# The branch behind the first attention, w_out beside the second: a hybrid transformer block on one core

## The chip, the cores and the metric

The kernel runs on one core of a Trainium2 chip. The metric is the time of one execution on the device in microseconds (us); the reported time is the median of several runs. The core has TensorE (PE, matmuls and transposes; PEld is its weight load), VectorE (DVE), ScalarE (ACT), GpSimd (POOL) and SyncE (SP, which only issues DMAs here; GpSimd issues some too). The engines run their own instruction streams and wait for each other by semaphores.

## The reference

One decoder block, 2048 tokens of width 1024, in fp32. Two head groups share one input projection, and their outputs go through one output projection:

```python
go = gla_chunked(gq, gk, gv, g_log)            # gated linear attention, 4 heads
go = from_heads(rms_norm(go, gla_norm)) * silu(g_og)
...
s1, s2 = (q_m @ k_m.T) * scale, causal         # two maps of each of 4 heads
p_diff = softmax(s1) - lam * softmax(s2)
do = from_heads(rms_norm(p_diff @ v, diff_norm) * (1 - lambda_init))
...
y = concat([go, do]) @ w_out
x = x + gate * rms_norm(y)
h = relu(modulate(rms_norm(x)) @ w_up) ** 2    # 4096 wide
x = x + gate2 * rms_norm(h @ w_down)
```

(Shortened; q, k have 64 columns for each map, v has 128.) The gated attention may use a short form where no gate decays too far; the kernel computes a flag from the data, and where it is set it runs a general form. In these inputs the flag is 0.

## The kernel before, in words

Every fp32 product is made of three matmuls on split operands (high x high, low x high, high x low). A weight is therefore split once: ScalarE casts its high part, VectorE subtracts it from the weight for the low part.

The first 800 us hold the normalisation, the input projections and the gated attention. Then come the two calls of the differential attention, written as a generator, `attention` (L175): the first (pool pA0, query blocks t = 0, 1 of 512 tokens), the second (pool pA1, t = 2, 3). A step is a head and 128 queries: score matmuls S (L218, two maps), their evacuation with the running minimum on VectorE (L223, and L226 for the masked block on the diagonal), exp on ScalarE (L236), the combination of the two maps on VectorE (L242), and two steps later the transposes PT (L267), their copy on ScalarE (L269) and the products O with V (L278). When a head's four steps are done, its norm runs (L293) and its transposes dps (L301) give the two-part result dmo, which goes to the DRAM tile mixS. The generator yields after each block of 512 keys: a step of t = 1 has two yields, of t = 2 three, of t = 3 four. S, PT and dps share four PSUM banks in turn, tag "C".

The order around the change is set by the program's order, by how many yields are run between other work (`run(at, n)`), and by a scheduler that moves instructions within the limits of their dependences; at a branch all instructions ahead of it stay ahead, and all behind it stay behind. The first attention's steps are run two yields at a time beside the last input projections (`AT0`); what is left of it stands behind the branch. The branch (L885) is the general gated attention. Not taken, each engine jumps to a join and first waits there for its own earlier instructions. Behind it w_out is loaded (eight tiles of 128x1024 by GpSimd's queue, L911, three buffers), and split (L920 on ScalarE, L921 on VectorE), with `WL` = 2 yields of the first attention ahead of each.

`out_proj` (L927) makes the output projection of a token tile (128 tokens): it loads mx from mixS (1 MB, L933, SP) and x (L935), then makes two halves of 8 x 3 matmuls Y (L943 to L945), with a yield after each three, and then the norm and the residual add (L948 to L963). `interleave` runs it beside attention by a rate (`RA` = 2 for the rest of the first attention, `RB` = 2 for 48 yields of the second, then `RC` = 1.5). Tiles go in the order `TOKS`; the first `TB` = 11 run beside attention, the other five behind it beside the loads and splits for the up projection. `prep_first` prepares the up projection's operand and is paced by the same count of steps.

Behind all this, from about 1310 us on, the up and the down projection of the MLP run; the change does not touch them.

Of the kernel before, what the change touches and what calls it, by code (L numbers as in the profile page):

```python
# [9 lines left out]
F32 = mybir.dt.float32  # L10
F32R = mybir.dt.float32r
# [3 lines left out]
ALU = mybir.AluOpType  # L15
# [4 lines left out]
P = 128  # L20
S = 2048
D = 1024
NK = D // P
NH = 4
# [10 lines left out]
AT0 = 2  # L35
GA1 = 4
WL = 2
RA = 2.0
RB = 2.0
RC = 1.5  # L40
GA0 = 22
# [8 lines left out]
def tile_hybrid_block(  # L50
# [3 lines left out]
    nc = tc.nc  # L54
# [12 lines left out]
    mixS = [dram.tile([P, 4, 2 * NH, 2, P], F32, name=f"mixS{t}") for t in range(NT)]  # L67
# [104 lines left out]
    finished = set()  # L172


    def attention(tlist, sb, pw, pb, pp, tags, kb_, vb_, lag):  # L175
        steps = [(t, h, j) for t in tlist for h in range(NH) for j in range(4)]
        heads, qts, tiles, outs, rsd = {}, {}, {}, {}, {}
        dmask = sb.tile([P, 512], F32, tag="dmask", name="dmask", bufs=1)
# [75 lines left out]
        def due():  # L254
            for e in [e for e in queue if e[0] <= tick[0]]:
                queue.remove(e)
                e[1](*e[2])
# [50 lines left out]
        n = len(steps)  # L308
        for s in range(n + lag):
            cur = steps[s] if s < n else None  # L310
            old = steps[s - lag] if s >= lag else None
            if cur is not None:
                for a in range(3):
                    load(steps[min(s + a, n - 1)])
                tiles[cur] = ([sb.tile([P, pw], F32, tag="P", name="P", bufs=pb) for _ in range(2)],
                              [sb.tile([P, 4], F32, tag="nm", name="nm", bufs=8) for _ in range(2)],
                              sb.tile([P, 2, 2], F32, tag="sums", name="sums", bufs=4))
            nq = cur[0] + 1 if cur is not None else 0
            np_ = old[0] + 1 if old is not None else 0
            for ci in range(max(nq, np_)):  # L320
                tick[0] += 1
                if ci < nq:
                    qk(cur, ci)
                due()
                if ci < np_:
                    turn(old, ci)
                yield
            if cur is not None:
                softmax(cur)
            if old is not None:  # L330
                del tiles[old]
        while queue:
            tick[0] += 1
            due()
            yield
# [6 lines left out]
    sb = c0.enter_context(tc.tile_pool(name="p0", bufs=2, side="left"))  # L342
    sg = cG.enter_context(tc.tile_pool(name="p0g", bufs=2, side="right"))
    cps = ExitStack()
    pp = cps.enter_context(tc.tile_pool(name="p0ps", bufs=1, space=PSUM))
# [100 lines left out]
    def run(g, n=None):  # L446

        while n is None or n > 0:
            if next(g, run) is run:
                return False  # L450
            n = None if n is None else n - 1
        return True
# [421 lines left out]
    cA = ExitStack()  # L874
    sa = cA.enter_context(tc.tile_pool(name="pA0", bufs=2, side="right", reuse_waits="tile"))
    atags = {"S": ("C", 4), "O": ("D", 2), "T": ("C", 4)}
    at = attention((0, 1), sa, 1024, 6, pp, atags, 3, 3, 2)
    while run(dp, 1):
        run(at, AT0)
    run(rest)  # L880
    c0.close()

    with tc.tile_pool(name="gc", bufs=1, side="left", reuse_waits="tile") as gc:
        flag = nc.values_load(fi[0:1, 0:1], min_val=0, max_val=P)
# [15 lines left out]

    c1 = ExitStack()
    sw = c1.enter_context(tc.tile_pool(name="p1w", bufs=2, side="left", reuse_waits="tile"))
    gtg = sw.tile([P, D], F32, tag="gtg", name="gtg", bufs=1)
    nc.gpsimd.dma_start(gtg, gtS[0].partition_broadcast(P))
    wohi, wolo, woraw = [], [], []

    def load_wo(k):
        raw = sw.tile([P, D], F32, tag="wx", name="woraw", bufs=3)  # L910
        nc.gpsimd.dma_start(raw, w_out[k * P:(k + 1) * P, :])  # L911
        woraw.append(raw)

    for k in range(3):
        load_wo(k)
    for k in range(NK):
        run(at, WL)
        wh = sw.tile([P, D], F32R, tag=f"wohi{k}", name="wohi", bufs=1)
        wl = sw.tile([P, D], F32R, tag=f"wolo{k}", name="wolo", bufs=1)
        nc.scalar.copy(wh, woraw[k])  # L920
        nc.vector.tensor_tensor(wl, woraw[k], wh.bitcast(F32), op=ALU.subtract)  # L921
        wohi.append(wh)
        wolo.append(wl)
        if k + 3 < NK:
            load_wo(k + 3)

    def out_proj(tiles):  # L927

        for tk in tiles:
            assert all((tk // 4, h) in finished for h in range(NH))  # L930
            mx = sw.tile([P, 2 * NH, 2, P], F32R, tag="mx", name="mx", bufs=2)
            for ks in (slice(0, 7), slice(7, 8)) if tk >= 12 else (slice(0, 8),):
                nc.sync.dma_start(mx[:, ks].bitcast(F32), mixS[tk // 4][:, tk % 4, ks])  # L933
            xt = sw.tile([P, D], F32, tag="wx", name="wxt", bufs=3)
            nc.sync.dma_start(xt, x[tk * P:(tk + 1) * P, :])  # L935
            yps = []
            ss = sw.tile([P, 2], F32, tag="wss", name="wss", bufs=2)
            for b in range(2):
                yp = pp.tile([P, 512], F32, tag=("C" if tk > 12 and tk % 2 else "A"), name="Y",
                             bufs=4 if tk > 12 and tk % 2 else 2)  # L940
                cs = slice(512 * b, 512 * b + 512)
                for k in range(NK):
                    nc.tensor.matmul(yp, mx[:, k, 0, :], wohi[k][:, cs], start=(k == 0), stop=False)  # L943
                    nc.tensor.matmul(yp, mx[:, k, 0, :], wolo[k][:, cs], start=False, stop=False)  # L944
                    nc.tensor.matmul(yp, mx[:, k, 1, :], wohi[k][:, cs], start=False, stop=(k == NK - 1))  # L945
                    yield
                junk = sw.tile([P, 512], BF16, tag="wjunk", name="wjunk", bufs=1)
                nc.scalar.activation(junk, yp, AF.Square, accum_out=ss[:, b:b + 1])  # L948
                yps.append(yp)
            s1 = sw.tile([P, 1], F32, tag="ws1", name="ws1", bufs=2)  # L950
            nc.vector.tensor_tensor(s1, ss[:, 0:1], ss[:, 1:2], op=ALU.add)
            r = rsqrt_col(sw, s1, 1, 1.0 / D, "wr")
            yt = sw.tile([P, D], F32, tag="wx", name="wyt", bufs=3)
            for b in range(2):
                cs = slice(512 * b, 512 * b + 512)
                nc.vector.scalar_tensor_tensor(yt[:, cs], yps[b], r, gtg[:, cs], op0=ALU.mult, op1=ALU.mult)
            eng = nc.vector if tk >= 11 else nc.gpsimd
            eng.tensor_tensor(xt, xt, yt, op=ALU.add)
            nc.gpsimd.dma_start(x1S[tk], xt)

            s2 = sw.tile([P, 1], F32, tag="ws2", name="ws2", bufs=2)
            nc.scalar.activation(yt, xt, AF.Square, accum_out=s2)
            r2 = rsqrt_col(sw, s2, 1, 1.0 / D, "wq")  # L963
            nc.vector.tensor_scalar(yt, xt, r2, None, op0=ALU.mult)
            nc.gpsimd.dma_start(xnS[tk // 8][:, tk % 8], yt.rearrange("p (k c) -> p k c", c=P))
# [6 lines left out]
    wdS = [dram.tile([P, 3, 512], F32, name=f"wdS{p}") for p in range(NP_)]  # L972

    TOKS = (0, 4, 1, 5, 2, 6, 3, 7) + tuple(range(8, 16))

    def prep_first(pool, tag):

# [28 lines left out]
            for _ in range(2):  # L1008
                yield


    TB = 11
    op = out_proj(TOKS[:TB])

    def interleave(at, first, rate, later, pre=None):


        due, i = 0.0, 0
        while run(at, 1):
            due += rate if i < first else later  # L1020
            while due >= 1.0:
                if len(wsteps) == 16 * TB or not ready(TOKS[len(wsteps) // 16]):
                    due = 0.0
                    break
                run(op, 1)
                wsteps.append(1)
                due -= 1.0
            if pre is not None:
                run(pre, 1)
            i += 1  # L1030

    wsteps = []

    def ready(tk):
        return all((tk // 4, h) in finished for h in range(NH))

    interleave(at, 0, RA, RA)
    cA.close()
    cA = ExitStack()
    sa = cA.enter_context(tc.tile_pool(name="pA1", bufs=2, side="right", reuse_waits="tile"))  # L1040
    at = attention((2, 3), sa, S, 6, pp, atags, 5, 5, 2)
    pre = prep_first(sa, "C")
    interleave(at, 48, RB, RC, pre)
    run(op)
# [53 lines left out]
    def fetch_op(m):  # L1098

        g, i = opseq[m]  # L1100
        hsrc[m] = [prep_tile("hsrc", [P, 2, 512]) for _ in range(2)]
        for kp in range(2):
            nc.sync.dma_start(hsrc[m][kp], hS[g][:, OP[i], 2 * kp:2 * kp + 2, :])
# [52 lines left out]

    op = out_proj(TOKS[TB:])
    fetch_op(0)
# [21 lines left out]
    pp = c3.enter_context(tc.tile_pool(name="p2ps", bufs=1, space=PSUM, reuse_waits="tile"))  # L1180
# [53 lines left out]
    n = len(usteps)  # L1234
    ready_ops = {}
    prep_todo = [(k, hf) for k in range(4) for hf in range(2)]
    for s, (g, c, wi, p) in enumerate(usteps):
        i = WORD[wi]
# [17 lines left out]
        nm, first = BANK[i]  # L1256
# [34 lines left out]
    pp = c4.enter_context(tc.tile_pool(name="p3ps", bufs=1, space=PSUM, reuse_waits="tile"))  # L1291
# [157 lines left out]
    banks = {}  # L1449
# [25 lines left out]
    for s in range(nd - TAIL):  # L1475
        if s + AHEAD < nd:
            ready_ops[s + AHEAD] = down_ops(s + AHEAD)
        i, p, gs = dsteps[s]
# [98 lines left out]
```

## Time and profile before

| what | us |
|---|---|
| median of 3 runs | 2572.22 |
| lowest, highest | 2565.59, 2573.88 |
| the profiled execution | 2572.86 |
| its span | 2570.7 |

The profiled execution's mean granted TensorE clock is 0.982. From about 801 to 1280 us the span holds what the change edits. In a row of a timeline stand the start, the duration, the engine, the line and the operation; in brackets the engine's idle time ahead of it and what ended it. A row of the windows has start and end, length, then the busy time of PE, PEld, DVE, ACT and POOL with the count of instructions, the granted clock of PE, the mean busy share of the 16 DMA engines, and GB/s. In rows of groups the busy time and the mean duration in ns stand first, then the idle time ahead of the group and what ended it.

### The profile page before, as it was taken

What the parts mean: (1) busy time and instruction counts of PE and PEld (TensorE: products, weight loads), DVE (VectorE), ACT (ScalarE), POOL (GpSimd) and SP (SyncE); (2) the same over time, 40 slices, a digit from 0 to 9 for tenths busy, and PEclk for the clock granted to TensorE, in tenths of its full rate; (3) what the DMA queues carried; (4) which work ended last, traced back from release to release, by engine and by line L of the source; (5) the groups of instructions that cost most, each with busy time, mean ns of one, the idle gap of its engine ahead of it and who ended that gap; (6) DMA issues with size and microseconds to landing.
All of it is one profiled execution on the core that took longest, in us unless ns stands there. A gap on an engine that the chain in (4) does not pass through costs nothing.

```text
span 2570.7 us, 35387 instructions
## 1 busy us (share of the span) xinstructions
PE 2457.0 (96%) x12532; PEld 2055.5 (80%) x12532; DVE 1589.8 (62%) x3111; ACT 1159.2 (45%) x2201; POOL 417.6 (16%) x638
## 2 busy tenths in 40 slices
PE   5999999999998899999999999999999999999998
PEld 4877788887787788888778888788888788788886
DVE  7536754347865677767576667766664445544756
ACT  4352224412545566556555555544553333222444
POOL 1011230003311123232012322212211000100000
PEclk8999999999999999999999999999999999999999
DMA  7354553244845667655565655734438767855856
GB/s 270 110 191 141 179 191 111 98 141 157 242 131 181 207 206 229 204 181 158 211 224 198 232 189 175 239 134 160 157 126 301 254 198 242 279 176 161 289 167 209
DMA packets 218791, 491.60 MB, mean 191 GB/s; under 512 B 24848, under 2 KB 78800, under 8 KB 217072
## 3 DMA queue, kind: packets, MB, share of 16 engines
q1 hardware_dynamic: 170000, 329.12, 40.5%
q0 software_dynamic: 48608, 160.16, 16.8%
q8 instruction: 100, 1.64, 0.3%
q14 instruction: 83, 0.68, 0.1%
HBM read 329.79 MB, written 159.39 MB: 190 GB/s over the span
## 4 chain that ended last, share of the span: by engine, by line
issue 34%; PE 23%; POOL 7%; DVE 2%; DMA 1%; ACT 1%; POOLq 0%; SPq 0%; DVEq 0%; ACTq 0%
PE dn L1440 5%; PE dn L1441 5%; PE dn L1442 4%; PE S L218 2%; PE O L278 2%; POOL uS L1222 2%; POOL uS L1191 2%; PE Y L945 1%; PE Y L944 1%; PE Y L943 1%; PE PT L267 1%; POOL wdS L1320 1%; POOL uS L1230 1%; ACT P L236 1%; DMA q<-qS 0%
## 5 line engine op out<-in xcount | busy, mean ns | idle before, releaser
L1440 PE MATMUL dn<-dnhi,uhi 128*128 128x512 f32 x880 | 344.5, 391 | 3.0 <-DVE du L1420 3.0
L1442 PE MATMUL dn<-dnhi,ulo 128*128 128x512 f32 x880 | 344.2, 391 | 2.0 <-DVE ulo L1369 2.0
L1441 PE MATMUL dn<-dnlo,uhi 128*128 128x512 f32 x880 | 344.1, 391 | 0.0
L1367 ACT CAST uhi<-us 128x1024 fp32r<-128x1024 f32 (+1 forms) x126 | 118.7, 944 | 357.9 <-PE dn L1441 341.4
L1369 DVE TENSOR_TENSOR ulo<-us,uhi 128x1024 fp32r<-128x1024 f32 (+1 forms) x126 | 137.0, 1087 | 158.6 <-ACT uhi L1367 158.3
L535 PE MATMUL projt<-hThi,whi 128*128 128x512 f32 x512 | 203.9, 398 | 1.1 <-DVE cols L420 0.6
L537 PE MATMUL projt<-hThi,wlo 128*128 128x512 f32 x512 | 201.5, 393 | 2.2 <-DVE wlo L476 2.2
L536 PE MATMUL projt<-hTlo,whi 128*128 128x512 f32 x512 | 201.4, 393 | 0.0
L1440 PEld LDWEIGHTS dn<-dnhi,uhi 128*128 128x128 f32 x880 | 165.9, 189 | 38.9 <-ACT dnhi L1366 2.8
L1442 PEld LDWEIGHTS dn<-dnhi,ulo 128*128 128x128 f32 x880 | 165.9, 189 | 37.6 <-DVE ulo L1369 2.4
L1441 PEld LDWEIGHTS dn<-dnlo,uhi 128*128 128x128 f32 x880 | 166.0, 189 | 35.3
L236 ACT ACTIVATE P<-P,nm 128x128 f32<-128x128 f32 (+15 forms) x128 | 153.7, 1202 | 48.8 <-DVE nm L226 46.1
L1145 ACT CAST wuhi<-wA 128x512 fp32r<-128x512 f32 x160 | 99.1, 619 | 165.3 <-PE upV L1264 67.0
L218 PE MATMUL S<-K,q 128*128 128x512 f32 (+3 forms) x640 | 169.5, 383 | 2.8 <-issue 1.5
L278 PEld LDWEIGHTS O<-V,PTs 128*128 128x128 f32 x1088 | 142.3, 193 | 25.4 <-ACT PTs L269 14.3
L278 PE MATMUL O<-V,PTs 128*128 128x128 f32 x1088 | 152.6, 281 | 7.9 <-ACT PTs L269 4.2
L550 PE MATMUL projn<-whi,hThi 128*128 128x256 f32 x512 | 150.5, 294 | 4.5 <-DVE cols L420 2.7
L1265 PE MATMUL upY<-hhi,wulo 128*128 128x512 f32 x384 | 151.9, 396 | 2.0 <-DVE wulo L1146 2.0
L1263 PE MATMUL upY<-hhi,wuhi 128*128 128x512 f32 x384 | 151.7, 395 | 0.0
L1264 PE MATMUL upY<-hlo,wuhi 128*128 128x512 f32 x384 | 151.4, 394 | 0.0
L552 PE MATMUL projn<-whi,hTlo 128*128 128x256 f32 x512 | 148.1, 291 | 0.3 <-DVE hTlo L168 0.3
L551 PE MATMUL projn<-wlo,hThi 128*128 128x256 f32 x512 | 148.2, 290 | 0.0
(334 smaller groups left out, 5713.9 us busy)
## 6 DMA issues: line engine op xcount, KB each, us to landing
us<-uS SPq DMA_DIRECT2D x94, 512.0 KB, 4.4
wA<-in_w_up_dram SPq DMA_DIRECT2D x128, 256.0 KB, 3.0
uS<-t POOLq DMA_DIRECT2D x128, 256.0 KB, 3.2
wraw<-in_w_in_dram SPq DMA_DIRECT2D x48, 512.0 KB, 4.6
uS<-c POOLq DMA_DIRECT2D x96, 256.0 KB, 3.1
K<-kS SPq DMA_DIRECT2D x40, 512.0 KB, 5.5
wds<-in_w_down_dram SPq DMA_DIRECT2D x78, 256.0 KB, 4.0
adaraw<-in_ada_w_dram SPq DMA_DIRECT2D x32, 512.0 KB, 4.1
```

What stands on the lines that cost most here:

```text
L218: nc.tensor.matmul(ps[:, :wd], qt[:, m, hl, qs], Kc[ci][:, m, :wd], start=(hl == 0), stop=(hl == 1))
L236: nc.scalar.activation(Ps[m][:, :width], Ps[m][:, :width], AF.Exp, scale=-1.0, bias=nms[m][:, t:t + 1], accum_out=sums[:, 0, m:m + 1])
L278: nc.tensor.matmul(outs[t, h][:, j, :], pt[:, kb % 4, :], Vc[g][:, kb % 4, :], start=(kb == 0), stop=(kb == nb - 1))
L535: nc.tensor.matmul(ps, whi[k][:, cs], hi[:, k, :], start=(k == 0), stop=False)
L536: nc.tensor.matmul(ps, whi[k][:, cs], lo[:, k, :], start=False, stop=False)
L537: nc.tensor.matmul(ps, wlo[k][:, cs], hi[:, k, :], start=False, stop=(k == NK - 1))
L1263: nc.tensor.matmul(ps, whi[:, k, :], hi[:, k, :], start=(first and k == 0), stop=False, skip_group_check=not first)
L1264: nc.tensor.matmul(ps, whi[:, k, :], lo[:, k, :], start=False, stop=False, skip_group_check=not first)
L1265: nc.tensor.matmul(ps, wlo[:, k, :], hi[:, k, :], start=False, stop=(k == 3), skip_group_check=not first)
L1440: nc.tensor.matmul(banks[t], uhi[:, tk], whi, start=first, stop=False, skip_group_check=on)
L1441: nc.tensor.matmul(banks[t], uhi[:, tk], wlo, start=False, stop=False, skip_group_check=on)
L1442: nc.tensor.matmul(banks[t], ulo[:, tk], whi, start=False, stop=last, skip_group_check=on)
```

## The change

All steps of the first attention are run ahead of the branch; only its queued end (the last products, the norm and the store) is left behind it. The pool of the second attention is opened right behind that, and the loads and splits of w_out are spread over the second attention's first 16 yields, where cast, subtraction and the first matmul of the output projection are kept in the order of the program. All 176 steps of the first eleven token tiles now run beside the second attention; before, the first tile's 16 ran beside the first. The load of mx goes through `load_mx`, one tile ahead of its use, x is loaded halfway through its tile, and for the last four tiles mx is loaded by GpSimd's queue. The PSUM banks of Y are "C" for tile 11, too (before: 13 and 15 only).

```diff
-RA = 2.0
...
-    def attention(tlist, sb, pw, pb, pp, tags, kb_, vb_, lag):
+    def attention(tlist, sb, pw, pb, pp, tags, kb_, vb_, lag, ends):
...
+        ends.append(tlist)
         while queue:
             tick[0] += 1
             due()
...
+    while not ends:
+        run(at, 1)
 
     with tc.tile_pool(name="gc", bufs=1, side="left", reuse_waits="tile") as gc:
         flag = nc.values_load(fi[0:1, 0:1], min_val=0, max_val=P)
...
+    run(at)
+    cA.close()
+    cA = ExitStack()
     c1 = ExitStack()
...
+    sa = cA.enter_context(tc.tile_pool(name="pA1", bufs=2, side="right", reuse_waits="tile"))
+    at = attention((2, 3), sa, S, 6, pp, atags, 5, 5, 2, ends)
+    run(at, 1)
     for k in range(3):
         load_wo(k)
     for k in range(NK):
         run(at, WL)
...
-        nc.scalar.copy(wh, woraw[k])
-        nc.vector.tensor_tensor(wl, woraw[k], wh.bitcast(F32), op=ALU.subtract)
+        tc.keep_in_program_order(nc.scalar.copy(wh, woraw[k]))
+        tc.keep_in_program_order(nc.vector.tensor_tensor(wl, woraw[k], wh.bitcast(F32), op=ALU.subtract))
...
+    def load_mx(tk):
+
+        if tk in mxs or not ready(tk):
+            return
+        mxs[tk] = sw.tile([P, 2 * NH, 2, P], F32R, tag="mx", name="mx", bufs=2)
+        eng = nc.gpsimd if tk >= 12 else nc.sync
+        for ks in (slice(0, 7), slice(7, 8)) if tk >= 12 else (slice(0, 8),):
+            eng.dma_start(mxs[tk][:, ks].bitcast(F32), mixS[tk // 4][:, tk % 4, ks])
+
     def out_proj(tiles):
 
         for tk in tiles:
-            assert all((tk // 4, h) in finished for h in range(NH))
-            mx = sw.tile([P, 2 * NH, 2, P], F32R, tag="mx", name="mx", bufs=2)
-            for ks in (slice(0, 7), slice(7, 8)) if tk >= 12 else (slice(0, 8),):
-                nc.sync.dma_start(mx[:, ks].bitcast(F32), mixS[tk // 4][:, tk % 4, ks])
-            xt = sw.tile([P, D], F32, tag="wx", name="wxt", bufs=3)
-            nc.sync.dma_start(xt, x[tk * P:(tk + 1) * P, :])
+            load_mx(tk)
+            mx = mxs.pop(tk)
+            banks = ("C", 4) if tk >= 11 and (tk - TB) % 2 == 0 else ("A", 2)
...
-                yp = pp.tile([P, 512], F32, tag=("C" if tk > 12 and tk % 2 else "A"), name="Y",
-                             bufs=4 if tk > 12 and tk % 2 else 2)
+                yp = pp.tile([P, 512], F32, tag=banks[0], name="Y", bufs=banks[1])
                 cs = slice(512 * b, 512 * b + 512)
                 for k in range(NK):
-                    nc.tensor.matmul(yp, mx[:, k, 0, :], wohi[k][:, cs], start=(k == 0), stop=False)
+                    mm = nc.tensor.matmul(yp, mx[:, k, 0, :], wohi[k][:, cs], start=(k == 0), stop=False)
+                    if (tk, b, k) == (0, 0, 0):
+                        tc.keep_in_program_order(mm)
...
+                    if (b, k) == (1, 0):
+
+                        xt = sw.tile([P, D], F32, tag="wx", name="wxt", bufs=3)
+                        nc.sync.dma_start(xt, x[tk * P:(tk + 1) * P, :])
+                        for nx in TOKS[TOKS.index(tk) + 1:TOKS.index(tk) + 2]:
+                            load_mx(nx)
                     yield
...
+    def op_step():
+
+        if len(wsteps) == 16 * TB or (len(wsteps) % 16 == 0 and TOKS[len(wsteps) // 16] not in mxs):
+            return False
+        run(op, 1)
+        wsteps.append(1)
+        return True
...
+            n = len(wsteps) // 16
+            if len(wsteps) % 16 == 0 and n < TB and TOKS[n] not in mxs:
+                load_mx(TOKS[n])
+                asked[n] = i
             while due >= 1.0:
-                if len(wsteps) == 16 * TB or not ready(TOKS[len(wsteps) // 16]):
+                n = len(wsteps) // 16
+                if (len(wsteps) % 16 == 0 and i < asked.get(n, -3) + 3) or not op_step():
                     due = 0.0
                     break
-                run(op, 1)
-                wsteps.append(1)
                 due -= 1.0
...
-    interleave(at, 0, RA, RA)
-    cA.close()
-    cA = ExitStack()
-    sa = cA.enter_context(tc.tile_pool(name="pA1", bufs=2, side="right", reuse_waits="tile"))
-    at = attention((2, 3), sa, S, 6, pp, atags, 5, 5, 2)
+    load_mx(0)
     pre = prep_first(sa, "C")
     interleave(at, 48, RB, RC, pre)
```

**SyncE's DMAs.** Before, SyncE (L206 is q, L933 mx, L196 V, L194 K, L935 x) has these rows behind the branch: the first mx and the last loads of the first attention, and then the second attention's K, V and q (kS_60, vS_64 and qS_62), which the scheduler moved into the first attention's time.

```order
L885 UNCONDITIONAL_BRANCH x2
L206 DMA q<-qS_63 64x2x256
L933 DMA mx<-mixS_78 128x2048
L196 DMA V<-vS_65 128x4x128
L194 DMA K<-kS_61 128x2x512
L206 DMA q<-qS_63 64x2x256 x4
L196 DMA V<-vS_65 128x4x128
L935 DMA wxt<-in_x_dram 128x1024 x2
L194 DMA K<-kS_60 128x2x512
L196 DMA V<-vS_64 128x4x128
```

In the change (L952 is mx, L193 K, L195 V, L205 q) the same place of SyncE reads:

```order
L889 UNCONDITIONAL_BRANCH x2
L952 DMA mx<-mixS_78 128x2048
L193 DMA K<-kS_60 128x2x512
L195 DMA V<-vS_64 128x4x128
L193 DMA K<-kS_60 128x2x512
L195 DMA V<-vS_64 128x4x128
L193 DMA K<-kS_60 128x2x512
L195 DMA V<-vS_64 128x4x128
L205 DMA q<-qS_62 64x2x256 x8
```

The loads of the first attention have moved ahead of the branch; the second attention's K, V and q now come right behind the join and the first mx.

**TensorE, the start of the second attention.** Before, TensorE has at the change from the first attention to the second: the last products of the first, its last dps, two steps of scores, and then the output projection's second token tile.

```order
L278 MATMUL O<-V,PTs 128x128 x8
L301 MATMUL dps<-ident,don 128x128 x4
L218 MATMUL S<-K,q 128x512 x8
L218 MATMUL S<-K,q 128x128 x4
L218 MATMUL S<-K,q 128x512 x8
L218 MATMUL S<-K,q 128x256 x4
L218 MATMUL S<-K,q 128x512
L943 MATMUL Y<-wohi,mx 128x512
L944 MATMUL Y<-wolo,mx 128x512
L945 MATMUL Y<-wohi,mx 128x512
```

In the change TensorE has at this place, right behind the join:

```order
L889 UNCONDITIONAL_BRANCH x2
L277 MATMUL O<-V,PTs 128x128 x5
L300 MATMUL dps<-ident,don 128x128 x4
L217 MATMUL S<-K,q 128x512 x8
L217 MATMUL S<-K,q 128x128 x4
L217 MATMUL S<-K,q 128x512 x8
L217 MATMUL S<-K,q 128x256 x4
L217 MATMUL S<-K,q 128x512 x4
L266 MATMUL PT<-ident,P 128x128 x4
L217 MATMUL S<-K,q 128x512 x4
```

The branch now stands ahead of the first attention's last five products, and no Y follows the first two steps of scores. The first Y of the change comes some fifty such rows later on TensorE, behind the scores of the sixth step:

```order
L217 MATMUL S<-K,q 128x512 x4
L277 MATMUL O<-V,PTs 128x128 x3
L266 MATMUL PT<-ident,P 128x128 x4
L217 MATMUL S<-K,q 128x512 x4
L277 MATMUL O<-V,PTs 128x128 x4
L266 MATMUL PT<-ident,P 128x128 x4
L217 MATMUL S<-K,q 128x256 x4
L277 MATMUL O<-V,PTs 128x128 x4
L266 MATMUL PT<-ident,P 128x128 x4
L966 MATMUL Y<-wohi,mx 128x512
L969 MATMUL Y<-wolo,mx 128x512
L970 MATMUL Y<-wohi,mx 128x512
```

Between the second attention's first scores and its first Y there are now only its own matmuls; VectorE has the eight subtractions of w_out (L931) among its work for the same steps.

More of the change, by code (lines that the diff above doesn't have):

```diff
@@ L876, in tile_hybrid_block @@
     atags = {"S": ("C", 4), "O": ("D", 2), "T": ("C", 4)}
-    at = attention((0, 1), sa, 1024, 6, pp, atags, 3, 3, 2)
+    ends = []
+    at = attention((0, 1), sa, 1024, 6, pp, atags, 3, 3, 2, ends)
     while run(dp, 1):
@@ L925, in tile_hybrid_block, with ready @@
             load_wo(k + 3)
+    TOKS = (0, 4, 1, 5, 2, 6, 3, 7) + tuple(range(8, 16))
+    TB = 11
+    mxs = {}
+    def ready(tk):
+        return all((tk // 4, h) in finished for h in range(NH))
+    def load_mx(tk):
[5 more added lines that the diff above has]
+            eng.dma_start(mxs[tk][:, ks].bitcast(F32), mixS[tk // 4][:, tk % 4, ks])
     def out_proj(tiles):
         for tk in tiles:
-            assert all((tk // 4, h) in finished for h in range(NH))
-            mx = sw.tile([P, 2 * NH, 2, P], F32R, tag="mx", name="mx", bufs=2)
-            for ks in (slice(0, 7), slice(7, 8)) if tk >= 12 else (slice(0, 8),):
-                nc.sync.dma_start(mx[:, ks].bitcast(F32), mixS[tk // 4][:, tk % 4, ks])
-            xt = sw.tile([P, D], F32, tag="wx", name="wxt", bufs=3)
-            nc.sync.dma_start(xt, x[tk * P:(tk + 1) * P, :])
+            load_mx(tk)
+            mx = mxs.pop(tk)
+            banks = ("C", 4) if tk >= 11 and (tk - TB) % 2 == 0 else ("A", 2)
             yps = []
@@ L972, in tile_hybrid_block @@
     wdS = [dram.tile([P, 3, 512], F32, name=f"wdS{p}") for p in range(NP_)]
-    TOKS = (0, 4, 1, 5, 2, 6, 3, 7) + tuple(range(8, 16))
     def prep_first(pool, tag):
@@ L1009, in prep_first, with interleave @@
                 yield
-    TB = 11
     op = out_proj(TOKS[:TB])
-    def interleave(at, first, rate, later, pre=None):
-        due, i = 0.0, 0
+    wsteps = []
+    def op_step():
[4 more added lines that the diff above has]
+        return True
+    def interleave(at, first, rate, later, pre):
+        due, i, asked = 0.0, 0, {}
         while run(at, 1):
             due += rate if i < first else later
+            n = len(wsteps) // 16
+            if len(wsteps) % 16 == 0 and n < TB and TOKS[n] not in mxs:
+                load_mx(TOKS[n])
+                asked[n] = i
             while due >= 1.0:
-                if len(wsteps) == 16 * TB or not ready(TOKS[len(wsteps) // 16]):
+                n = len(wsteps) // 16
+                if (len(wsteps) % 16 == 0 and i < asked.get(n, -3) + 3) or not op_step():
                     due = 0.0
                     break
-                run(op, 1)
-                wsteps.append(1)
                 due -= 1.0
-            if pre is not None:
-                run(pre, 1)
+            run(pre, 1)
             i += 1
-    wsteps = []
-    def ready(tk):
-        return all((tk // 4, h) in finished for h in range(NH))
-    interleave(at, 0, RA, RA)
-    cA.close()
-    cA = ExitStack()
-    sa = cA.enter_context(tc.tile_pool(name="pA1", bufs=2, side="right", reuse_waits="tile"))
-    at = attention((2, 3), sa, S, 6, pp, atags, 5, 5, 2)
+    load_mx(0)
     pre = prep_first(sa, "C")
```

## Prediction

> **What bounds the kernel now.** I read the totals first, then the busy time by stretch around the edited code, then TensorE's own timeline there. The profiled execution took 2572.86 us with a span of 2570.7 us; the median shown is 2572.22, so sums made against this execution stand 0.6 us above the median.
>
> ```profile
> span 2570.7 us, 35387 instructions
> PE 2457.0 (96%) x12532; PEld 2055.5 (80%) x12532; DVE 1589.8 (62%) x3111; ACT 1159.2 (45%) x2201; POOL 417.6 (16%) x638
> ```
>
> TensorE (PE) is busy 96% of the span. The change leaves the count of matmuls as it is, so it can only win or lose PE's idle or slow-clocked time. The stretches show where that lies around the branch (columns: window, length, busy time of PE, weight loads, VectorE, ScalarE, GpSimd, granted clock, DMA share, GB/s).
>
> ```profile
> 801.50:863.30 61.80, 46.48 (x269) 38.86 (x269) 41.49 (x116) 38.31 (x93) 9.72 (x14) 0.88 0.72 231
> 863.30:875.00 11.70, 9.14 (x32) 7.40 (x33) 8.99 (x29) 5.66 (x8) 2.23 (x4) 0.75 0.64 227
> 875.00:1235.00 360.00, 350.68 (x2145) 304.36 (x2144) 263.79 (x762) 217.28 (x436) 95.17 (x116) 0.99 0.60 192
> 1050.00:1060.00 10.00, 7.61 (x31) 5.62 (x29) 9.75 (x28) 6.30 (x21) 2.93 (x2) 0.83 0.60 179
> 1135.00:1145.00 10.00, 7.95 (x40) 6.59 (x38) 7.05 (x19) 4.88 (x10) 1.10 (x2) 0.83 0.38 139
> ```
>
> From 875 to 1235 PE is busy 350.68 of 360 us at clock 0.99: with output-projection matmuls (Y) as filler, the second attention is bound by PE. From 801.5 to 863.3, the rest of the first attention with the split of w_out, it is busy 46.48 of 61.80 at clock 0.88. PE's timeline shows the waits in there.
>
> ```profile
> 804.78 0.76 PE L278 MATMUL O<-V,PTs 128*128 128x128 f32 x2 [3.23 <-PEq L885]
> ...
> 854.80 2.05 PE L278 MATMUL O<-V,PTs 128*128 128x128 f32 x16 [0.24 <-ACT PTs L269]
> 863.32 1.09 PE L301 MATMUL dps<-ident,don 128*128 128x128 f32 x4 [6.47 <-DVE don L293]
> 864.05 1.20 PE L218 MATMUL S<-K,q 128*128 128x512 f32 x2
> ...
> 874.37 0.50 PE L943 MATMUL Y<-wohi,mx 128*128 128x512 f32 x1 [2.38 <-DMA mx<-mixS]
> ```
>
> The branch costs 3.23 us; the last head's norm chain, between its last O and dps, 6.47. The first score matmuls (S) of the second attention follow dps at once: their loads had long landed. At 874.37 the second attention's first Y runs, with two steps of S behind it. That is my fixed point: I work out when the changed kernel reaches its first Y, and put the work that is then ahead or behind into microseconds of PE.
>
> **Part 1, the first attention alone.** In the change the six remaining steps of the first attention run before the branch, without Y and without the split. VectorE (DVE) sets their pace.
>
> ```profile
> L921 DVE TENSOR_TENSOR wolo<-woraw,wohi 128x1024 fp32r<-128x1024 f32 x8 | 9.7, 1218 | 2.1 <-ACT wohi L920 2.1
> L956 DVE SCALAR_TENSOR_TENSOR wyt<-Y,wrr,gtg 128x512 f32<-128x512 f32 x2 | 1.4, 746 | 0.0
> ```
>
> DVE is busy 41.49 us between 801.5 and 863.3. Less the eight split subtractions (9.7) and Y's evacuation (1.4) that is 30.4 for the first attention; about 2 of it is the last head's norm, which stays behind the branch. So 28.4 us from 801.5, then transposes, copy and O of the last step (about 1.5): 831.5 if DVE never idles. I take 833 for its idling; at the share of the row 863.30:875.00 (8.99 of 11.70) it would be 838. The branch itself goes nowhere: every engine still waits at the join for its own earlier work, 3.23 as before. The join is at about J = 836.
>
> **Part 2, from the join to the first S.** Before, K, V and q of the second attention were issued while the first one still ran:
>
> ```profile
> 843.71 0.54 SPq L194 DMA_DIRECT2D K<-kS  x1
> 844.30 0.59 SPq L196 DMA_DIRECT2D V<-vS  x1
> ```
>
> That is 20 us ahead of the S that used them (864.05). In the change they stand behind the branch on SyncE (SP), behind the first mx load, and GpSimd's queue issues gtg and three pieces of w_out at the same moment. Sizes and one full stretch:
>
> ```profile
> K<-kS SPq DMA_DIRECT2D x40, 512.0 KB, 5.5
> q<-qS SPq DMA_DIRECT2D x128, 128.0 KB, 4.5
> mx<-mixS SPq DMA_DIRECT2D x12, 1024.0 KB, 5.6
> V<-vS SPq DMA_DIRECT2D x40, 256.0 KB, 4.1
> woraw<-in_w_out_dram POOLq DMA_DIRECT2D x8, 512.0 KB, 6.5
> ...
> 815.00:820.00 5.00, 3.03 (x8) 1.92 (x8) 3.57 (x10) 4.16 (x6) 0.53 (x1) 0.80 0.99 342
> ```
>
> Ahead of the fourth piece of q, which S needs, SP has mx, three K, three V and four q: 1024+1536+768+512 = 3840 KB. GpSimd has three pieces of w_out and gtg, a 128x1024 fp32 tile like them: 2048 KB. At 342 GB/s, where the DMA share is 0.99, the 5888 KB (6.03 MB) take 17.6 us. From below, S cannot start before the norm chain has let dps go: O about 1.1, then 6.47, then 0.73 to the first S, so J+8. I take J+16, near the burst, because not all of GpSimd's bytes need to be ahead of q: 852. The ends J+8 and J+18 are kept.
>
> The Trainium skill (Trainium Kernel Development and Optimization, "Key Constraints") says that transfers issued from different engines' queues run on the same 16 DMA engines and interleave. It speaks against this change, which puts both queues' bursts at one point. Were the queues independent, SP's 3840 KB alone would take 11.5 us and the sum would be 4 us lower; with the rule it stands. The trace has no such burst of this size; its row above has both queues near saturation.
>
> **Part 3, the second attention without filler.** The w_out split now lies in its first 16 yields, and the first Y is held behind the scores of the sixth step. Until then PE has 72 S matmuls, 42 transposes and 38 products O.
>
> ```profile
> 876.56 0.39 PE L943 MATMUL Y<-wohi,mx 128*128 128x512 f32 x1
> 876.79 0.40 PE L944 MATMUL Y<-wolo,mx 128*128 128x512 f32 x1
> ...
> 888.08 1.08 PE L218 MATMUL S<-K,q 128*128 128x512 f32 x4
> 889.00 1.05 PE L278 MATMUL O<-V,PTs 128*128 128x128 f32 x8
> 889.89 0.60 PE L267 MATMUL PT<-ident,P 128*128 128x128 f32 x4
> 890.24 0.47 PE L943 MATMUL Y<-wohi,mx 128*128 128x512 f32 x1
> ```
>
> By the distances of these starts a Y takes 0.23 us, four S of 512 columns 0.92, four O (which the trace lists as eight) 0.89, four transposes 0.35. So 12 full yields of S make 11.0, the six partial ones 128+256+384+512+128+256 = 1664 columns, 3.0; O 8.5; transposes 3.7: 26 us of PE. DVE has more to do:
>
> ```profile
> L223 DVE TENSOR_SCALAR_CACHE_REDUCE P<-S,nm 128x512 f32<-128x512 f32 x10 | 7.2, 747 | 1.0 <-PE S L218 1.0
> L223 DVE TENSOR_SCALAR_CACHE_REDUCE P<-S 128x512 f32<-128x512 f32 x10 | 6.5, 689 | 6.2 <-PE S L218 6.1
> L242 DVE SCALAR_TENSOR_TENSOR P<-P,cf 128x1152 f32<-128x1152 f32 (+3 forms) x4 | 6.5, 1616 | 0.0
> L226 DVE CUSTOM_DVE_ANT_0 P<-S,dmask,nm 128x128 f32<-128x128 f32 (+3 forms) x8 | 4.1, 545 | 2.5 <-PE S L218 2.5
> L223 DVE DVE_READ_ACCUMULATOR P<-S 128x1 f32 x10 | 0.8, 83 | 0.0
> ```
>
> The last transposes ahead of Y take the bank of a score tile whose evacuation is 24th in DVE's order. Up to there: 12x0.747 + 12x0.689 = 17.2; 10x0.545 = 5.5; 34 accumulator reads at 0.083 = 2.8; five L242 at 1.616 = 8.1; five times some 0.5 of one-column work = 2.6; seven subtractions at 1.218 = 8.5. That is 44.7 us. The reads lie partly beside other work, DVE idles a little, so I take 45, from 43 to 58 (44.7 at the share 8.99/11.70). The first Y is at 852 + 45 = 897.
>
> By then the changed kernel is ahead in attention: 26.2 us of PE against the two steps of S done by 874.37 (4.4), so 21.8. It is behind by one token tile of Y, since before that tile ran beside the first attention: 48 x 0.23 = 11.0. Net 10.8 us, 11 at the pace of the long stretch (360/350.68). So 897 stands for 886, against 874.4: **11.6 us late**.
>
> **Part 4, the rest of the second attention and the tail.** Before, the Y tiles ended early and the attention's end ran without them; now they reach to its end, so nothing more is due later. Two holes may close.
>
> ```profile
> 1128.15 0.47 SPq L935 DMA_DIRECT2D wxt<-in_x_dram  x1
> ```
>
> ```profile
> 1134.71 1.06 ACT L962 ACTIVATE wyt<-wxt 128x1024 f32<-128x1024 f32 x1 [2.66 <-POOL wxt L958]
> ```
>
> In 1135:1145 PE lost 3.4 us (10 - 7.95x0.83). Just ahead of it ScalarE waited 2.66 us for a tile's residual add, whose x was asked for at 1128.15 only, late on SP behind the loads of mx and K; mx is now asked for a tile earlier, and x half a tile ahead of its use. In 1050:1060 it lost 3.7, where Y waits for banks. I take 2 back (ends 0 and 7). The tail's bank wait goes, since tile 11 takes other banks:
>
> ```profile
> 1252.99 0.79 PE L943 MATMUL Y<-wohi,mx 128*128 128x512 f32 x1 [2.80 <-DVE wyt L956]
> ```
>
> But tile 12 now fills the drain of the last head and follows tile 10 in the same banks. I take 2 back (0 to 2.8).
>
> **Sum:** 11.6 - 2 - 2 = +7.6, so 2572.9 + 7.6 = 2580.5; less the 0.6 to the median I say **2580**. Prefetching mx takes PE's 2.38 us wait at 874.37 away, but in the change that time lies inside the DVE-bound stretch, so I count it at nothing; if Y began earlier it would be worth that much.
>
> **Rivals.**
> First, *the loads hide*: S follows dps at J+8, as before. First Y 836+8+45 = 889, stands for 878, 3.6 late; less 4 it is -0.4: 2572.5. For it: 20 us of lead were more than needed, and K alone lands in 5.5. Against: SP serves mx first, and 5.9 MB at once.
> Second, *it really gains*: the same, DVE at 43, both holes and the tail wait closed: 836+8+43-11 = 876, 1.6 late, less 7 and 2.8: -8.2, or 2564.5. For it: those holes are waits that prefetching meets. Against: 1050:1060 is a bank wait with DVE busy 9.75 of 10, which the change doesn't touch.
> Third, *slower by more*: DVE idles in the unfilled stretch as it does in 863.30:875.00, since each S waits for a bank and each transpose for ScalarE, which also casts w_out: 58 instead of 45, +13 more: 2593. It decides as soon as DVE's share there is below 0.85. Against: with Y as filler the long stretch shows no such waits.
>
> The Trainium skill (TensorE: Matmul & The Clock Gate, "A second HAM failure mode: psum-queue depth-cycling") tells of PE dropping to half clock when it idles often and briefly while cycling through banks; by that the 26 us of PE would be 52 in the unfilled stretch, which also gives about 7 us more than my sum. Here clock 0.75 in 863.30:875.00 follows a long idle, so the trace leaves it open, and I count it under the third rival.
>
> **Chances.** The forecast (burst, DVE-bound start) 0.45; loads hidden 0.28; a real gain 0.12; slower by more 0.15. About 0.3%, 7.7 us, can be told from no change. The forecast's own range, +2 to +12, lies on both sides of that: 0.19 of it within, 0.26 above. Hence faster 0.12, same 0.28+0.19 = 0.47, slower 0.26+0.15 = 0.41. The range goes from the second rival's 2564 to just short of the third's 2593.
>
> **What would show it.** PE's timeline: the branch wait near 833 and still about 3 us; the first S of the second attention at least 12 us behind the join, released by a DMA (if by dps, the first rival); DVE's share above 0.9 from there to the first Y, PE's near 0.6; the first Y some 45 us after the first S; no 2.8 us wait at the tail. I am wrong if the first Y comes before 885 or if the stretch behind it loses much less than the 9.3 us idle of now.

## The result and the profile after

The change makes the kernel slower: a median of 2594.26 us (4 runs, 2589.53 to 2606.09) against 2570.4 us of before, ratio 1.0095 with a 95% interval of 1.0071 to 1.0119. Later, on another chip, it was 2597.45 against 2570.38, ratio 1.0117 (1.0100 to 1.0134). The forecast was 2580, its range 2564 to 2592.

The page of the changed kernel: the same matmuls, the same busy time of TensorE, a longer span.

```profile
span 2588.3 us, 35407 instructions
PE 2456.2 (95%) x12532; PEld 2053.4 (79%) x12532; DVE 1585.2 (61%) x3111; ACT 1158.3 (45%) x2201; POOL 422.9 (16%) x646
```

Its stretches, in the columns of before:

```profile
797.00:825.00 28.00, 23.66 (x147) 20.88 (x146) 19.10 (x64) 16.63 (x40) 1.26 (x2) 0.88 0.35 104
825.00:855.00 30.00, 16.79 (x108) 14.74 (x106) 13.82 (x42) 14.83 (x41) 3.29 (x6) 0.80 0.41 133
855.00:875.00 20.00, 6.70 (x20) 5.41 (x20) 4.62 (x14) 2.70 (x4) 1.13 (x3) 0.53 0.93 279
875.00:900.00 25.00, 20.76 (x108) 15.36 (x107) 24.06 (x66) 17.15 (x26) 2.69 (x5) 0.93 0.76 232
```

From 825 to 875 TensorE is busy 23.5 of 50 us; from 875 to 900 VectorE is full (24.06 of 25) and TensorE is not. The waits that make this, in TensorE's timeline of the changed kernel:

```profile
810.29 1.11 PE L300 MATMUL dps<-ident,don 128*128 128x128 f32 x4 [3.37 <-DVE don L292]
...
831.69 0.63 PE L300 MATMUL dps<-ident,don 128*128 128x128 f32 x4 [2.25 <-DVE sums L238]
...
841.36 0.94 PE L277 MATMUL O<-V,PTs 128*128 128x128 f32 x6 [0.29 <-ACT PTs L268]
845.79 1.70 PE L277 MATMUL O<-V,PTs 128*128 128x128 f32 x10 [3.50 <-PEq L889]
851.68 1.08 PE L300 MATMUL dps<-ident,don 128*128 128x128 f32 x4 [4.19 <-DVE don L292]
868.30 8.19 PE L217 MATMUL S<-K,q 128*128 128x512 f32 x24 [15.53 <-DMA q<-qS]
...
909.18 0.48 PE L966 MATMUL Y<-wohi,mx 128*128 128x512 f32 x1
```

TensorE comes to the branch at 842.3 and leaves the join at 845.8; the first S of the second attention runs at 868.30, after 15.53 us of waiting for q; the first Y at 909.18. The executions of one kernel differ among themselves in the MLP's phases, so I compare the start of the last Y, the end of what the change edits. These numbers are the first and last starts in the views of the tiles S, Y and dn:

| profile | first S | first Y | last Y | first dn | span |
|---|---|---|---|---|---|
| before | 648.2 | 816.4 | 1300.8 | 1939.3 | 2570.7 |
| before, a second profile (c4) | 647.9 | 814.6 | 1299.2 | 1932.0 | 2560.9 |
| changed | 648.9 | 909.2 | 1324.3 | 1958.8 | 2588.3 |
| changed, a second profile (a1) | 650.8 | 910.1 | 1324.5 | 1961.1 | 2600.3 |

The last Y is 23.5 us later, and about as much in the second pair (25.3): that is the median's difference of 24 and 27 us. Behind it the same kernel's two profiles differ by 8 us (before) and 12 us (changed). The one execution of before that the prediction was summed against took longer over the up projection: 638.5 us from its last Y to its first dn, 632.8 in the second. In all the profiles of this document the first S lies between 646.2 and 653.5 us, though no edit touches the code ahead of it; so a difference of a few us between the last Y of single profiles proves little.

### The profile page after: what moved, and what is told of

Its sections match the earlier page's. It is cut to its first block, busy times and chain, and to the rows that moved or that the text cites. A ratio compares the mean times of both kernels' runs of the same rounds, so it can differ in the third digit from the quotient of the medians.

```text
span 2588.3 us, 35407 instructions
## 1 busy us (share of the span) xinstructions
PE 2456.2 (95%) x12532; PEld 2053.4 (79%) x12532; DVE 1585.2 (61%) x3111; ACT 1158.3 (45%) x2201; POOL 422.9 (16%) x646
## 4 chain that ended last, share of the span: by engine, by line
PE 47%; issue 11%; DVE 3%; DMA 2%; POOL 2%; ACT 2%; SPq 1%; DVEq 0%; POOLq 0%; ACTq 0%
PE dn L1472 6%; PE dn L1470 6%; PE dn L1471 6%; PE S L217 3%; PE upY L1295 3%; PE upY L1294 3%; PE upY L1293 3%; PE O L277 3%; PE upX L1293 2%; PE upX L1294 2%; PE upX L1295 2%; PE upV L1295 2%; PE upV L1294 2%; PE upV L1293 2%; PE Y L970 1%
```

## The experiments

Ratios are against the kernel before on the same chip, with their 95% intervals.

**The change again, and the kernel before again.** Two measurements of the noise.

> The changed kernel again, on the chip of the next three. Its profiled execution was 17 us above that of before, its median 24 us. If the profile shows the whole cost, 0.6 to 0.8% (15 to 20 us) here; if something differs from one execution to the next beyond the profile, up to 0.95%.

> The kernel before once more, for a second profile: how far its phases differ from one execution to the next. From the first S to the first dn within 2 us of 1291.1; the phase from the first dn to the end between 629 and 634 us if the changed kernel's 639 in one of two is its own, or up to 640 if that phase varies by itself.

a1: 1.0117 (1.0100 to 1.0134), above the 0.95% that I had written as its upper end. c4, one time only: 2562.89 us. Its phase from the first S to the first dn was 1284.1 us, not within 2 us of 1291.1 as I had written, and from the first dn to the end it took 628.9. The table above holds both: up to the last Y the profiles of one kernel agree within 2 us, behind it not.

**The branch back at its old place, all else as changed** (a2; d2 also with the old banks for Y).

```diff
-    while not ends:
-        run(at, 1)
     with tc.tile_pool(name="gc", ...
         ...
+    while not ends:
+        run(at, 1)
     run(at)
```

> The changed kernel with the branch back ahead of the first attention's remaining steps, all else as changed. Theory A (the join bars the second attention's loads): K, V and q are issued during the first attention again, the 15.5 us wait of the first S goes, of which some 4 us norm chain and cold clock remain; 10 to 14 us faster than the changed kernel. Theory B (what costs is the missing filler and the split at the second attention's start; the branch is indifferent): within 4 us of the changed kernel.

> The changed kernel with branch and banks both as before. If the causes add, 0.43% less 0.36%: within 0.2% of before. If the lost filler costs something of its own, 0.2 to 0.5% above before.

a2: 1.0043 (1.0023 to 1.0063); d2: 1.0041 (1.0025 to 1.0058). TensorE of a2 around the first S:

```profile
855.75 1.09 PE L300 MATMUL dps<-ident,don 128*128 128x128 f32 x4 [4.19 <-DVE don L292]
856.49 0.78 PE L217 MATMUL S<-K,q 128*128 128x512 f32 x1
```

S follows dps at once, since its loads went out during the first attention. The first Y comes at 898.0, 11.2 us earlier than in the changed kernel, and by the medians a2 is 16 us below a1. Theory A holds, a little above its 10 to 14. From the first S to the first Y it still takes 41.5 us, as in the changed kernel (40.9): the length of that stretch does not depend on where the branch stands. d2 shows no gain by the banks here.

**No branch at all** (b3 of the changed kernel, b4 of the kernel before; both leave out the general gated attention, which these inputs don't take).

> The changed kernel without the general gated attention and its branch (not taken with these inputs). Theory A (the join bars loads and stalls): 16 to 22 us faster than the changed kernel. Theory B: only the 3.5 us stall goes, 3 to 6 us.

> The kernel before without the general gated attention and its branch. The stall of 3.2 us, the 1.5 us behind it and some of the cold clock go, and w_out can be loaded earlier, so its 2.2 us wait goes too: 6 to 10 us faster than before. With the run before it this gives the price of the branch at either place.

b3: 1.0002 (0.9986 to 1.0019), last Y at 1307.4. b4: 0.9991 (0.9978 to 1.0004), last Y at 1301.4. So the branch is worth 0.9 to 1.2% (24 to 30 us) in the changed kernel, against its two measurements and above what Theory A said, and nothing that can be told in the kernel before; there I had expected 6 to 10. TensorE of b4 tells why:

```profile
811.99 0.58 PE L278 MATMUL O<-V,PTs 128*128 128x128 f32 x2 [4.87 <-DMA V<-vS]
817.80 0.76 PE L923 MATMUL Y<-wohi,mx 128*128 128x512 f32 x1 [5.23 <-DMA mx<-mixS]
```

Without the stall TensorE runs into the loads of V and mx instead (4.87 and 5.23 us). So it seems that the branch at its old place costs only what those waits would have cost anyway. And without a branch the missing filler, the split at the second attention's start and the new projection code together cost nothing that the times can tell (b3). One thing speaks against nothing at all: in b3's one profile the last Y comes 6 to 8 us later than in the two profiles of before.

**The burst in order** (b1; d3 with the old banks).

```diff
-        nc.gpsimd.dma_start(raw, w_out[k * P:(k + 1) * P, :])
+        if k < 3: tc.keep_in_program_order(nc.sync.dma_start(raw, ...))
+        else: nc.gpsimd.dma_start(raw, ...)
...
+    tc.keep_in_program_order(nc.sync.dma_start(gtg, ...))
+    load_mx(0)   # its DMA kept in program order, too
```

> The changed kernel with the burst behind the join put in order: the first mx, gtg and three pieces of w_out go out on SyncE behind the second attention's first K, V and q. If the wait of the first S is the bytes ahead of its q, S comes about 12 us behind the join instead of 22.5 (2.8 MB at 0.34 to 0.38 MB per us and some latency) and the kernel is 6 to 10 us faster than changed. If the wait is issue or latency of the queue, S moves by less than 4 us. A loss elsewhere: the split waits for w_out, up to 5 us back.

> The changed kernel, branch late, with the burst behind the join put in order (b1) and the banks as before. By adding: 0.70% less 0.36%, 0.3 to 0.4% above before. If the banks are harmless here: 0.6 to 0.75%.

```profile
845.98 1.78 PE L277 MATMUL O<-V,PTs 128*128 128x128 f32 x10 [3.16 <-PEq L889]
851.94 1.08 PE L300 MATMUL dps<-ident,don 128*128 128x128 f32 x4 [4.19 <-DVE don L292]
859.01 7.13 PE L217 MATMUL S<-K,q 128*128 128x512 f32 x24 [5.98 <-DMA q<-qS]
```

```profile
850.96 7.49 SPq L205 DMA_DIRECT2D q<-qS  x8
```

TensorE of b1 has the same join, and S 13 us behind it instead of 22.5, close to the 12 written for the bytes; 1.0070 (1.0048 to 1.0091), 0.25 and 0.47% below the changed kernel's two measurements, which were made on other chips and whose intervals touch it. Its last Y comes at 1313.7, 10.6 us earlier. So what stands on the queues ahead of q makes the wait of the first S. Whether it does so by its bytes on the DMA engines or by holding up SyncE's issuing, b1 can't tell, because the edit takes away both: SyncE issued its first piece of q 5.0 us behind the join here (850.96) and 12.1 us behind it in the changed kernel (857.89), so some 7 of the 9.5 us lie in that, and the rest in a quicker landing. d3: 1.0053 (1.0036 to 1.0070), between what the two theories of its banks say.

**An earlier first Y** (b2: `WL = 1`).

> The changed kernel with one yield (not two) of the second attention ahead of each split, so that Y starts at its ninth yield. If the start is bound by VectorE's evacuations and subtractions, the first Y comes some 15 us earlier in the second attention and the time falls by 3 to 6 us, since the subtractions now crowd together; if Y's absence costs nothing, within 2 us.

1.0088 (1.0057 to 1.0118). The first Y comes at 894.4, 14.8 us earlier, as expected, but the last Y stays at 1325.0 (1324.3 in the changed kernel). Filling the second attention's start earlier gains nothing up to the end of Y. The eight subtractions crowd into 21 us there (874.4 to 895.6); whether that takes the gain back was not tested.

**The split back beside the first attention** (a3: branch early, w_out loaded and split beside the first attention's rest, its own Y still in the second).

> Branch early as in the run before, and w_out loaded and split beside the first attention's rest; only the first token tile's Y stays in the second attention. Theory A: no more than 3 us below the run before, since the loads were all that cost. Theory B: the start of the second attention is no longer bound by VectorE and its first Y comes at its first yields; 6 to 10 us below the run before and within 5 us of the kernel before.

1.0057 (1.0040 to 1.0074), no better than a2. The first Y comes at 871.4, 26.6 us before a2's, but the last Y at 1316.3 against 1313.8: the split lengthens the first attention's rest (the second one's first S comes at 869.2 against 856.5) and saves no more than that behind it. Theory B fell here.

**The new projection code alone** (a4, and again as c1: the kernel before with the changed out_proj, load_mx and interleave; c2 with the last four tiles' mx on SyncE; c3 with the old banks; d1: the changed kernel with the old banks).

```diff
-            banks = ("C", 4) if tk >= 11 and (tk - TB) % 2 == 0 else ("A", 2)
+            banks = ("C", 4) if tk > 12 and tk % 2 else ("A", 2)
```

> The kernel before with the changed out_proj, load_mx and interleave alone (mx asked for a tile ahead, x halfway, tile 11 in banks C). The prediction's part 4 says 4 us faster than before, between 0 and 10; with the tail's 2.8 us bank wait gone. A rival: the new waits (three yields after a late mx, tile 12 behind tile 10) give it back, 0 to 3 us slower.

> The kernel before with the changed projection code alone, a second time. Its first profile stood 0.7 us above before from the first S to the first dn, its median 10 us. If that median was a matter of few executions, it is now within 4 us of before; if the code costs time that the first profile does not hold, 8 to 14 us above it again, and this profile shows in which phase.

> As the run before, with the mx loads of the last four tiles on SyncE again and not on GpSimd's queue. If the queue is at fault (the 5.48 us wait of the tail's Y for mx behind GpSimd's stores), that wait is below 2 us and the median falls by 3 us or more; if not, within 2 us of it.

> As the first of this call, with the banks of Y as before (tile 11 in A). If the banks are the gain of the tail, the 2.8 us bank wait is back and the time is 2 to 4 us above the first; if the banks hardly matter, within 2 us.

> The changed kernel with Y's banks as before (tile 11 in A). If the bank term is the same as in the kernel before (c1 against c3: 0.36%), 8 to 10 us below the changed kernel, some 0.75% above before. If the other filler of the changed kernel's tail (tile 10 is there, and its wait for mx was 1.85 us instead of 5.48) makes the banks harmless, within 3 us of the changed kernel, 1.0% above before.

a4: 1.0053 (1.0030 to 1.0076); c1: 1.0031 (1.0016 to 1.0045), 7 us above before and between the two cases that I had written; c2: 1.0034 (1.0021 to 1.0046); c3: 0.9995 (0.9981 to 1.0009). Tile 11 in banks C costs some 0.36 to 0.58% against c3, where I had counted a gain. TensorE of a4, then of c3, in the tail:

```profile
1272.42 0.77 PE L955 MATMUL Y<-wohi,mx 128*128 128x512 f32 x1 [5.48 <-DMA mx<-mixS]
```

```profile
1249.98 0.50 PE L955 MATMUL Y<-wohi,mx 128*128 128x512 f32 x1 [2.81 <-DVE wyt L974]
...
1257.45 0.50 PE L955 MATMUL Y<-wohi,mx 128*128 128x512 f32 x1 [1.05 <-DMA mx<-mixS]
```

The bank wait goes, as said, but now tiles 11 and 12 run side by side, both mx buffers stay taken until the first of the two is done, and the next tile's mx is asked for only then. GpSimd's queue in a4:

```profile
1263.98 1.07 POOL L941 DMA_DIRECT2D mx<-mixS  x2 [6.52 <-PE Y L957]
```

These loads take 8.3 and 8.6 us to land, and Y starts at 1272.42, when they have. GpSimd's queue is not to blame for the time: in c2 the 5.48 us are gone, a bank wait of 2.17 stands there instead, and the time is that of c1. So the wait for the buffer is read from the trace and not shown to be the cost. A third mx buffer, which would test the buffers by themselves, wasn't tried, for want of on-chip memory beside the second attention's pool. d1: 1.0071 (1.0056 to 1.0086), below both measurements of the changed kernel, but its profile's last Y (1325.0) is no earlier than the changed kernel's, and d2 shows nothing. What the banks cost inside the changed kernel stays open between 0 and 0.46%.

## Why the prediction was wrong

The sign was right, and so was the burst behind the join as a cause; the sum, +7.6 us, was too small by some 16. The term that failed first is **J**, the join (9.8 us), then the wait for the first S (6.5 us), and then the 4 us that Part 4 took back. That the missing filler is lost time was part of the forecast's mechanism, and the runs do not bear it out.

- **Part 1, the first attention alone.** I took VectorE's 28.4 us of work as the pace, allowed 1.5 us for its idling, and put TensorE's arrival at 833 (838 with VectorE's share of 863.30:875.00). It was 842.3, a join at 845.8 instead of 836: 9.8 us too early. The work was as summed, the idling was not:

```profile
801.50:842.30 40.80, 33.21 (x207) 29.51 (x205) 28.24 (x90) 25.55 (x63) 1.44 (x2) 0.87 0.27 81
```

  VectorE was busy 28.24 us and idle 12.6, where the forecast had 3.1 in all (its idling, and the last transposes and products). No engine is full there. TensorE's rows point to chains of waits: a dps that holds the scores queued behind it (3.37 and 2.25 us), the low clock behind each of them (0.50 in 811.0:813.5 and in 833.0:835.5), and the last two steps' transposes and products with no scores beside them (836 to 842). What each of these costs was not tested.
- **The branch.** 3.50 us of TensorE; forecast 3.23.
- **Part 2, join to first S.** I took J+16 and J+18 as its upper end; it was J+22.5, 6.5 us more. The burst was there (b1), its size was off: the forecast went by bytes at one rate and counted nothing for SyncE's issuing, but q went out only 12.1 us behind the join, and the rate fell at the end, as the last section shows. (The first S, at 868.30, follows the landing of q's second piece, at 868.2; I had counted four pieces ahead of it.) The Trainium skill's rule on the shared DMA engines (Trainium Kernel Development and Optimization, "Key Constraints"), weighed there, agrees as far as the runs go: in 856:861 SyncE's queue took 62.6% and GpSimd's 43.0% of the 16 DMA engines' time, which is the row's share of 1.06. By the forecast's sum independent queues would have given J+12; the changed kernel had J+22.5, and b1, with GpSimd's bytes and mx taken from ahead of q, had J+13. What mx did and what the other queue did was not separated.
- **Part 3, first S to first Y.** 40.9 us; forecast 45, ends 43 to 58. The stretch of the changed kernel, columns as above:

```profile
868.00:909.00 41.00, 36.02 (x188) 28.27 (x189) 37.53 (x96) 25.79 (x38) 2.69 (x5) 0.89 0.70 217
```

  VectorE was the bound: it was busy 37.53 of 41 us, the share above 0.9 that the prediction named. The durations of its rows there add up to 44.6 us, much as I had summed them, but they overlap by some 7. My TensorE share of 0.6 was wrong (36.02 of 41). The lower clock, 0.89, explains a part of that: 36.02 x 0.89 is 32.1, against the 26 us that I had summed. The rest was not followed.
- First Y: 9.8 + 6.5 - 4.1 = 12.2 us later than forecast, 909.2 against 897.
- **Part 4.** Forecast: 4 us back. From the first Y of the second attention to the last Y it took 426.4 us before (1300.8 - 874.4) and 415.1 in the changed kernel; the 11 us of work by which that was ahead account for all of it, so nothing came back. The prefetch may help (c3 has the lowest last Y of all, 1294.8, but its time cannot be told from before). The banks did the opposite of what I counted: the wait for banks turned into one for buffers. So 12.2 and 4 are the 16 us.
- **Rivals.** The third, slower by more, came nearest in time (2593), but not by its mechanism: VectorE did not idle in the second attention's start. The half-clock mechanism of the Trainium skill (TensorE: Matmul & The Clock Gate, "A second HAM failure mode: psum-queue depth-cycling") did not show either: the clock was 0.93 in 875:900. That section tells of a clock that swings between half and full, so the 52 us that I put it at were its far end. The clock here fell once, to 0.63 in 880:883 behind a wait of 2.14 us, and was 1.00 from 886 on, amid waits of 0.16 to 0.58 us.
- Not seen at all: without a branch the missing filler costs nothing that the times can tell (b3). I had counted the hole at the second attention's start as lost time; b2 and a3, which have their first Y earlier, end no earlier. The branch at its old place still costs 0.4% where the first attention's rest has no filler (a2 against b3), and nothing that can be told where it has (before against b4). In a2 that loss arises in the first 20 us behind the branch and stays: its first dps behind the branch comes at 819.40 against 813.48 in b3, its first Y at 898.0 against 891.4, its last Y at 1313.8 against 1307.4. Why filler would hide it was not followed further.

## What to carry to other kernels

A branch that all engines join is a wall for prefetch: count not the stall but every load that the scheduler had moved across that place, and the order in which the loads then share the DMA engines. A stretch whose filler is taken away can run at the pace of its chain of waits, which the sum of its busiest engine's work does not give: here 28.24 us of work took 40.8, while the second attention's start did keep VectorE full. And when a wait for one buffer is lifted, look for the next one of the same tile: here, by the trace, the wait for a bank became one for an operand buffer.

## What the runs showed of the hardware that was not expected

The burst behind the join in the changed kernel, by stretch:

```profile
846.00:856.00 10.00, 2.58 (x14) 1.91 (x13) 2.26 (x7) 3.02 (x11) 3.50 (x7) 0.53 0.98 338
856.00:861.00 5.00, 0.00 (x0) 0.00 (x0) 0.00 (x0) 1.04 (x1) 0.20 (x1) 0.50 1.06 383
861.00:866.00 5.00, 0.00 (x0) 0.00 (x0) 0.00 (x0) 0.00 (x0) 0.00 (x0) 0.50 1.04 239
```

With the DMA engines as busy, the rate falls from 383 to 239 GB/s when the pieces of q (64 partitions, 128 KB each) come last. The packets are smaller there: 1426 packets for 1.20 MB in 861:866, against 1290 for 1.91 MB in 856:861. So the smaller packets cost more of the DMA engines' time per byte here. SyncE itself was held up as well:

```profile
845.77 0.55 SPq L193 DMA_DIRECT2D K<-kS  x1
...
849.25 6.16 SPq L193 DMA_DIRECT2D K<-kS  x1
855.46 2.39 SPq L195 DMA_DIRECT2D V<-vS  x1
857.89 9.94 SPq L205 DMA_DIRECT2D q<-qS  x8
```

The third K took 6.16 us to issue, where the first took 0.55; so q went out only 12.1 us behind the join. The eight pieces of q then took 9.94 us, more than 1 us each. In the kernel before they took as long, at a DMA share of 1.05 (847.5:857.0), but beside other work of TensorE:

```profile
847.47 9.14 SPq L206 DMA_DIRECT2D q<-qS  x8
```

Whether a full queue did that was not tested by itself.
